# Joining the opening, the queues and the tail of an encoder kernel: seven sets of small moves

## The chip, the cores and the metric

The kernel runs on one core of a Trainium2 chip. A core has a matrix engine (TensorE, PE in the profile), VectorE (DVE), ScalarE (ACT), GpSimd (POOL) and SyncE (SP), which works in order like the others and here mostly issues DMAs. PSUM, where TensorE writes, has eight banks. The metric is device time in microseconds of one execution; less is better. The kernel before takes 2608.68 us, the median of three runs (2608.54 to 2611.68).

## The reference

The reference is one layer of a bidirectional encoder, on two sequences of 2048 tokens of width 1024 with shared weights:

- `u = rmsnorm(h)`, then one projection `z = u @ w_in` to 2304 columns, cut into q (512), k and v (128 each), attention gate `ga` (512), Fourier input `f` (512) and Fourier gate `gf` (512).
- Group A: grouped-query attention with 8 query heads and 2 key/value heads of 64, with normalised q and k and axial rotary positions, softmax over all 2048 keys, times `silu(ga)`.
- Group B: the real part of a 2-D DFT over positions and the 64 channels of each of 8 groups, then a 64 x 64 map per group, times `silu(gf)`.
- `h = h + concat(A, B) @ w_out`; then `h + (p @ w_ple) * sigmoid(rmsnorm(h) @ w_ple_gate)`, with `p` the embedded rows of width 256; a last RMS norm.

## The kernel before, in words

Products with 16-bit operands are made as three, from a high and a low half of each operand (`SPLIT3`); a value is scaled to a power of two, cast by ScalarE to its high half, and VectorE subtracts that from the value to get the low half ("split").

**Stage one, the opening (`project`, L607).** A chunk is two tiles of 128 tokens; there are 16, eight a sequence. Each `iteration(i)` (L849) holds work on several chunks at once: it loads x of chunk i+4, normalises and splits chunk i+2 (`hi_u`, `lo_u`, transposed by DMA into `uc`), projects chunk i to q and k, v (`mm_tile`), norms and rotates chunks i-1 and i-2 (`norm_q`, `rope_q`, GpSimd and VectorE), splits q and k of i-3 (`lo_q`), and between these pieces advances the sweep of chunk i-1 (`sweep_part`, the projections to f, gf and ga with their gates). Chunks other than the first of a sequence are folded: GpSimd adds the two halves of `uc` (`fold_u`), then forms sum and difference of the two tiles (`fold_s`), and ScalarE and VectorE split these (`fold_hl`) into `uf`, which the next iteration's sweep reads. Half h = 0 holds k tiles 0 to 3, half 1 the rest. Every fifth step of a sweep advances a background generator (`bg`): it scales the output weights, then the embedded rows (`embed_rows`, L440), then the channel map. Every few steps another generator, `ahead`, runs the first row maxima of the attention (`maxima(..., first=True)`, L1318), each with two PSUM banks of its own. All engines run in the order in which the text writes them.

`vs` holds v of a chunk in two buffers. `late` (L722) takes its maximum and puts its store on the list `stores_next`, which the start of the next iteration issues on SP together with the stores of the transposed q and k.

**Stage two, the attention.** 64 units of 128 queries and one key/value head, eight steps each: scores, exponentials on ScalarE (L1302), sums of these on GpSimd (L1305, L1307), a row maximum 14 steps ahead on VectorE (L1337), values (L1365); at the fifth step of the next unit the sums are made (L1381) and divided (L1388). Between the steps `interleave` puts as much of a filler as a budget in us allows: the second DFT stage with the channel map (`fourier2`), then the output stage. `mix_scale` finds the scale of the output stage, once for each sequence. `hook` (L1937) loads output weights, at every other one of its calls. In this stage all but GpSimd run in the order of the text; GpSimd's order is a planner's, by costs and readiness.

**Stage three, the output (`outp`).** For each tile t: `out1` (the product with `w_out`, two column groups), `out3` (the gate product, two groups), `middle` (squares and norm), `out2` and `out4` (the split for the gate, the last norm and store). In `slot` (L1586) a group is held: its products are made with the upper 64 rows of the array while the lower 64 rows finish the group before. From t = 30 on (`WHOLE`) a group is made at once, after the held one has been finished with the lower rows alone. A copy of one column into `seen` makes TensorE wait for what has been written. What the filler has not done when the attention ends is drained with PSUM's banks regrouped (`psD`), and there the planner orders all engines. Tile 31 needs the last unit's result, which goes to memory and comes back as `ag`.

Of the kernel before, what the change touches and what calls it, by code (L numbers as in the profile page):

```python
# [10 lines left out]
F32 = mybir.dt.float32  # L11
# [154 lines left out]
class Build:  # L166
# [146 lines left out]
    def mul1(self, name, a, b):  # L313
        t = self.keep(name, [128, 1])
        self.nc.vector.tensor_tensor(out=t[:], in0=a, in1=b, op=ALU.mult)
        return t
# [123 lines left out]
    def embed_rows(self, pool):  # L440
# [12 lines left out]

        load(0)
        yield
        load(1)
        yield
        for i in range(NT):
            load(i + 2)
            x, b = tl.pop(i), self.pb[:, 2 * i:2 * i + 2]  # L460
            nc.vector.tensor_reduce(out=b, in_=x[:], op=ALU.max, axis=AX.X, apply_absolute_value=True)
            nc.vector.tensor_scalar(out=b, in0=b, scalar1=1e-30, scalar2=None, op0=ALU.max)
            nc.vector.tensor_scalar(out=b.bitcast(I32), in0=b.bitcast(I32), scalar1=0x7F800000,
                                    scalar2=None, op0=ALU.bitwise_and)
            f = st.tile([128, 2], F32, name="p_f")
            nc.vector.tensor_scalar(out=f[:].bitcast(I32), in0=b.bitcast(I32), scalar1=-1,
                                    scalar2=(254 + W_EXP) << 23, op0=ALU.mult, op1=ALU.add)
            yield
# [138 lines left out]
    def project(self, P, PU, W, early, later, wkv, wq, wf, wgf, wga, bg, mid):  # L607
# [99 lines left out]
        def mm_tile(i, tt):  # L707
# [14 lines left out]
            def late():  # L722
                nc.vector.tensor_reduce(out=self.vmax[s][:, t:t + 1], in_=pkv[:, 128:256], op=ALU.max, axis=AX.X,
                                        apply_absolute_value=True)
                stores_next.append(lambda: nc.sync.dma_start(
                    self.vd[s][:, :, t, :].rearrange("v p d -> p v d"), vs[:, tt]))
            VL[i, tt] = late

        def norm_q(i, rs):
            rope_tables(i)  # L730
            QN[i] = qn = P.tile([128, CH, 10, 64], F32, name="qn", bufs=1)
            nc.gpsimd.tensor_tensor(out=qn[:], in0=Z[i][0][:], in1=rs[:].unsqueeze(3).to_broadcast([128, CH, 10, 64]),
                                    op=ALU.mult)
            T1[i] = t1 = P.tile([128, CH, 10, 64], F32, name="t1", bufs=2)
            rt = RT[i]
            for _, sl, nh, g in heads:
                nc.gpsimd.tensor_tensor(out=t1[:, :, sl, :], in0=qn[:, :, sl, :],
                                        in1=rt[:, g, :, 0:64].unsqueeze(2).to_broadcast([128, CH, nh, 64]),
# [1279 lines left out]
```

## Time and profile before

| | |
|---|---|
| median of three runs | 2608.68 us |
| profiled execution | 2608.45 us |
| its span, first to last instruction | 2606.7 us |
| TensorE busy | 2513.0 us, 96% |
| VectorE, ScalarE, GpSimd busy | 65%, 45%, 72% |
| mean granted TensorE clock | 0.990 |
| the opening, about | 0 to 766 us |
| attention with its fillers, about | 766 to 2512 us |
| what is left of the output stage, about | 2512 to 2607 us |

In a row of the timeline stand the start, the duration, the engine, the line, the operation, what is written and read, the count, and in square brackets the time for which the engine was idle before it, with what ended that wait. In a row of waits stand who waited for whom, the total in us, how often, and the longest. In a row of the windows stand, after the stretch, its length and the busy time of PE, PE's weight load, DVE, ACT and POOL, and then the granted clock, the busy share of the DMA engines and GB/s.

### The profile page before, as it was taken

How to read it: one execution, taken by the hardware profiler on the slowest of the kernel's cores; microseconds unless marked ns; L12 is line 12 of the kernel's file. 1: busy time of each engine (PE TensorE's matmuls, PEld its weight loads, DVE VectorE, ACT ScalarE, POOL GpSimd, SP SyncE). 2: the span in 40 equal slices, each digit the busy share in tenths (PEclk: the TensorE clock that was granted, in tenths of full speed). 3: DMA queues.
4: the chain of work that ended last, by engine and by line, in shares of the span. 5: the costliest groups of instructions: out<-in, count | busy, mean ns of one | idle time of the engine just before them, and what ended most of it. 6: DMA issues, size and time to landing. Idle time of an engine off the chain costs nothing. (4 is left out here: it accounts for less than half of the span.)

```text
span 2606.7 us, 49785 instructions
## 1 busy us (share of the span) xinstructions
PE 2513.0 (96%) x19896; PEld 1384.8 (53%) x19896; DVE 1707.0 (65%) x2318; ACT 1183.6 (45%) x1983; POOL 1879.2 (72%) x1570
## 2 busy tenths in 40 slices
PE   6999999999889999999999999999999999999998
PEld 3566666666556545545545455444544555545543
DVE  7877676887566856566676666566666666666534
ACT  4443444343235545555444455544544444444531
POOL 1466454555549988888889888887888988888850
PEclk9999999999999999999999999999999999999999
DMA  8467697876267732222222323322223222232322
GB/s 258 102 183 190 196 247 212 197 169 174 87 178 243 222 116 59 61 64 74 68 70 69 80 65 99 88 60 78 70 74 84 72 68 70 66 82 74 80 77 51
DMA packets 450601, 297.92 MB, mean 114 GB/s; under 512 B 294000, under 2 KB 394736, under 8 KB 450368
## 3 DMA queue, kind: packets, MB, share of 16 engines
q1 hardware_dynamic: 438512, 257.00, 38.3%
q0 software_dynamic: 11856, 37.74, 4.0%
q8 instruction: 155, 2.54, 0.4%
q14 instruction: 78, 0.64, 0.1%
HBM read 146.12 MB, written 82.45 MB: 88 GB/s over the span
## 5 line engine op out<-in xcount | busy, mean ns | idle before, releaser
L1307 POOL TENSOR_TENSOR acc<-acc,p 128x1024 f32<-128x1024 f32 x384 | 929.2, 2420 | 112.9 <-ACT p L1302 86.6
L1337 DVE TENSOR_REDUCE a_mx<-ps_m 128x1 f32<-128x1024 f32 x498 | 608.9, 1223 | 515.8 <-PE ps_m L1329 504.4
L1302 ACT ACTIVATE p<-ps_s,s_scale 128x512 f32<-128x512 f32 x1024 | 648.1, 684 | 641.0 <-PE ps_s L1299 628.0
L1626 PE MATMUL ps_g<-w_pg,hT 64*128 64x512 f16 x2784 | 496.5, 377 | 5.9 <-DVE seen L1592 5.4
L1365 PE MATMUL ps_o<-p,v 128*64 128x256 f32 x4096 | 468.2, 381 | 0.0
L1299 PE MATMUL ps_s<-q,k 64*128 64x512 f16 x3072 | 432.0, 377 | 1.4 <-ACT p L1302 1.0
L1365 PEld LDWEIGHTS ps_o<-p,v 128*64 128x64 f32 x4096 | 283.7, 137 | 160.0 <-issue 28.1
L491 PEld LDWEIGHTS <-uc 128*128 128x128 f16 x2400 | 235.8, 98 | 230.9 <-DMA uc<-hl 20.0
L1626 PEld LDWEIGHTS <-hT 64*128 64x128 f16 x2784 | 205.2, 94 | 160.4 <-issue 19.9
L1626 PE MATMUL ps_g<-w_wo,mh 64*128 64x512 f16 x1440 | 260.3, 376 | 2.8 <-DVE mh L1536 1.5
L1626 PE MATMUL ps_g<-w_wo,mT 64*128 64x512 f16 x1440 | 257.4, 376 | 0.2 <-DMA mT<-mh 0.2
L1299 PEld LDWEIGHTS <-k 64*128 64x128 f16 x3072 | 152.6, 94 | 194.8 <-issue 76.2
L1329 PE MATMUL ps_m<-k,q 64*128 64x512 f16 x996 | 200.5, 377 | 16.0 <-DVE a_mx L1337 15.9
L491 PEld LDWEIGHTS <-w_ga 128*128 128x128 f16 x1536 | 152.4, 100 | 45.9 <-issue 22.6
L1305 POOL TENSOR_TENSOR acc<-p,p 128x1024 f32<-128x1024 f32 x64 | 151.0, 2359 | 17.2 <-ACT p L1302 16.5
L1626 PEld LDWEIGHTS <-mh 64*128 64x128 f16 x1440 | 101.6, 94 | 91.1 <-issue 16.8
L1626 PEld LDWEIGHTS <-mT 64*128 64x128 f16 x1440 | 107.1, 94 | 76.6 <-issue 4.8
L754 POOL TENSOR_TENSOR t<-t,t 128x1280 f32<-128x1280 f32 x16 | 46.2, 2889 | 114.2 <-DVE t L750 114.2
L491 PE MATMUL ps_x<-uc,w_ga 128*128 128x256 f16 x1008 | 116.2, 276 | 4.4 <-DVE a_mx L1337 3.3
L1388 DVE RECIPROCAL ps_f<-ps_f 128x256 f32<-128x256 f32 x62 | 108.9, 1756 | 13.6 <-PE ps_f L1381 13.6
L491 PE MATMUL ps_x<-w_gf,uc 128*128 128x512 f16 x480 | 105.9, 379 | 2.5 <-DVE a_mx L1337 2.5
L1073 POOL DMA_DIRECT2D agd<-gat x64 | 35.3, 552 | 101.2 <-DVE gat L1083 96.4
(336 smaller groups left out, 3424.5 us busy)
## 6 DMA issues: line engine op xcount, KB each, us to landing
q<-qTd SPq DMA_DIRECT2D x256, 64.0 KB, 2.2
ag<-agd SPq DMA_DIRECT2D x64, 256.0 KB, 3.3
out<-h POOLq DMA_DIRECT2D x31, 512.0 KB, 3.1
x<-in_x_prompt SPq DMA_DIRECT2D x16, 512.0 KB, 4.7
gfd<-gt POOLq DMA_DIRECT2D x32, 256.0 KB, 2.6
agd<-gat POOLq DMA_DIRECT2D x64, 128.0 KB, 3.0
w_st<-in_w_out SPq DMA_DIRECT2D x32, 256.0 KB, 4.0
w_st<-in_w_ple_gate SPq DMA_DIRECT2D x32, 256.0 KB, 4.1
```

The lines of the kernel that those rows point to most:

```text
L491: self.nc.tensor.matmul(ps, lhs(ia, k), rhs(ib, k), start=(i == 0), stop=(i == 3 * ks - 1))
L754: nc.gpsimd.tensor_tensor(out=t1[:], in0=t1[:], in1=t2[:], op=ALU.add)
L1073: nc.gpsimd.dma_start(self.agd[s][1, r * 128:(r + 1) * 128, c * n:(c + 1) * n], gt[:, :n])
L1299: nc.tensor.matmul(S[u][e][:], w[sl], q[sl].rearrange("p h q -> p (h q)"), start=j == i == 0, stop=i + 1 == len(todo), skip_group_check=True)
L1302: nc.scalar.activation(p[:, e, :], S[u][e][:], AF.Exp, scale=self.sc["s_scale"][:])
L1305: nc.gpsimd.tensor_tensor(out=ACC[u][:], in0=P[u, 0][:], in1=p[:], op=ALU.add)
L1307: nc.gpsimd.tensor_tensor(out=ACC[u][:], in0=ACC[u][:], in1=p[:], op=ALU.add)
L1329: nc.tensor.matmul(ps[c], Q[u][0][sl, h, :], kt[s, kv, half][sl, :, 0, :], start=True, stop=True)
L1337: nc.vector.reduce_max(MX[u][:, h, half, c:c + 1], x, axis=AX.X)
L1365: nc.tensor.matmul(o[64 * f:64 * f + 64], vt[s, kv, c // 8][:, c % 8, :], p[:, e, f], start=(c == 0), stop=(c == 15))
L1388: nc.vector.reciprocal(r, r)
L1626: nc.tensor.matmul(g[0][:], g[1](ia, k)[sl], g[2](ib, k)[sl], start=a, stop=z, skip_group_check=True)
```

## The change

- `embed_rows`: the scale of a step's rows is made one step ahead (`scale(i + 1)`), in operations on one column instead of two; the transpose is issued a step after the low half.
- `late`: from chunk 2 on the store of v is issued at once; the second tile's is at the start of the iteration, ahead of the loads.
- `norm_q`, `rope_q`, `fold_u`: GpSimd's operations over a chunk are made tile by tile.
- `iteration`: half 0 of the folded rows is split after 12 instead of 8 us of sweep, half 1 after all of it. In the last iteration the stores of q and k are issued on GpSimd's queue (before, the switch came after them).
- `sweep_ga`: the last chunk's gates are made in the place of the k/v weights, which are done with.
- `maxima`: the first memset is on VectorE. `mul1` and one line of `mix_scale` become tensor-scalar operations.
- attention: the last unit's sums go to the bank of the maxima. `hook` loads nothing in its first four calls.
- `slot`: where a group is made whole, it comes before the rest of the held one. `norm`: on VectorE from step 512 on. `prep`: tile 31 is split after the products of tile 30.

```
 mul1:
-        self.nc.vector.tensor_tensor(out=t[:], in0=a, in1=b, op=ALU.mult)
+        self.nc.vector.tensor_scalar(out=t[:], in0=a, scalar1=b, scalar2=None, op0=ALU.mult)
 embed_rows:
+        def scale(i):
+            x, b = tl[i], self.pb[:, 2 * i:2 * i + 2]
+            nc.vector.tensor_reduce(out=b, in_=x[:], op=ALU.max, axis=AX.X, apply_absolute_value=True)
+            f = st.tile([128, 2], F32, name="p_f", bufs=2)
+            cs = [(b[:, t:t + 1], f[:, t:t + 1]) for t in range(2)]
...
+        scale(0)
+        yield
         for i in range(NT):
             load(i + 2)
-            x, b = tl.pop(i), self.pb[:, 2 * i:2 * i + 2]
...
+            x, f = tl.pop(i), fs.pop(i)
             hl = pool.tile([128, 2, 2, 256], F16, name="p_hl", tag="w2k", bufs=self.nw2k)
             for t in range(2):
                 nc.scalar.activation(hl[:, t, 0, :], x[:, t, :], AF.Copy, scale=f[:, t:t + 1])
             yield
+            if i + 1 < NT:
+                scale(i + 1)
...
+            yield
             pT = pool.tile([128, 2, 4, 128], F16, name="p_T", tag="w2k", bufs=self.nw2k)
 mm_tile, late:
-                stores_next.append(lambda: nc.sync.dma_start(
-                    self.vd[s][:, :, t, :].rearrange("v p d -> p v d"), vs[:, tt]))
+                store = lambda: nc.sync.dma_start(self.vd[s][:, :, t, :].rearrange("v p d -> p v d"), vs[:, tt])
+                if i < 2:
+                    stores_next.append(store)
+                else:
+                    store()
 norm_q:
-            nc.gpsimd.tensor_tensor(out=qn[:], in0=Z[i][0][:], in1=rs[:].unsqueeze(3).to_broadcast([128, CH, 10, 64]),
-                                    op=ALU.mult)
+            for tt in range(CH):
+                nc.gpsimd.tensor_tensor(out=qn[:, tt], in0=Z[i][0][:, tt], op=ALU.mult,
+                                        in1=rs[:, tt].unsqueeze(2).to_broadcast([128, 10, 64]))
...
 rope_q:
-            nc.gpsimd.tensor_tensor(out=t1[:], in0=t1[:], in1=t2[:], op=ALU.add)
+            for tt in range(CH):
+                nc.gpsimd.tensor_tensor(out=t1[:, tt], in0=t1[:, tt], in1=t2[:, tt], op=ALU.add)
 fold_u:
-            nc.gpsimd.tensor_tensor(out=FT[h][:], in0=x(0), in1=x(1), op=ALU.add)
+            for tt in range(CH):
+                x = [U[i][:, tt, b, 4 * h:4 * h + 4, :].rearrange("p k r -> p (k r)") for b in range(2)]
+                nc.gpsimd.tensor_tensor(out=FT[h][:, tt], in0=x[0], in1=x[1], op=ALU.add)
 iteration:
+            if ok(i - 1) and i > 2:
+                VL.pop((i - 1, 1))()
+            if i == n + 3:
+                self.last_stores = nc.gpsimd
             if ok(i + 4):
                 load_x(i + 4, 0)
...
-            if ok(i - 1) and i > 2:
-                VL.pop((i - 1, 1))()
...
                 fold_u(i, 1)
-                sweep_part(8.0)
+                sweep_part(12.0)
                 fold_hl(i, 0)
                 fold_s(i, 1)
-                sweep_part(7.0)
+            sweep_part(1000.0 if i < n else (6.0, 9.0, 5.0, 100.0)[i - n])
+            if folds(i):
                 fold_hl(i, 1)
-            sweep_part(1000.0 if i < n else (6.0, 9.0, 5.0, 100.0)[i - n])
 sweep_ga:
+        g8 = self.gat8() if (s, c) == (1, NT // 2 - 1) else None
-            gt = w2k("gat")
+            gt, th = (w2k("gat")[:, :n], w2k("th")) if g8 is None else (g8[:, 2 * r], g8[:, 2 * r + 1])
 maxima:
-                    nc.gpsimd.memset(MX[u][:], -3e38)
+                    nc.vector.memset(MX[u][:], -3e38)
 attention:
-                    ps = self.bank()
+                    ps = self.bank() if u < n else self.psM.tile([128, 1024], F32, name="ps_m")
 mix_scale:
-        nc.vector.tensor_tensor(out=b[:], in0=b[:], in1=mm[:, 2:3], op=ALU.max)
+        nc.vector.tensor_scalar(out=b[:], in0=b[:], scalar1=mm[:, 2:3], scalar2=None, op0=ALU.max)
 slot:
-            if low is not None and (low[4] or whole):
+            def seen():
                 j = st.tile([128, 1], F32, name="seen")
                 nc.vector.tensor_copy(j[:], low[0][:, 0:1])
+            if low is not None and low[4] and not whole:
+                seen()
...
-            if low is not None:
-                yield from halves(None, low)
             if up is not None:
                 ps = self.group_bank()
                 for i, us in enumerate(self.mm(ps[:], up[0], up[1])):
                     yield us
                     yield from embed(i >= 6)
+                if low is not None:
+                    seen()
                 yield from self.after(ticket)
                 yield from end(up[2](ps))
+            if low is not None:
+                yield from halves(None, low)
 norm:
-            e = nc.vector if self.dq is None or t == 0 else nc.gpsimd
+            e = nc.vector if self.dq is None or t == 0 or self.step >= 16 * N2 else nc.gpsimd
 prep:
-            while MB == 1 and t - 1 in M:
+            while (MB == 1 and t - 1 in M) or (t == N2 - 1 and not free):
                 yield None
 outp:
+                if t == N2 - 2:
+                    free.append(True)
 run:
-                    W[n] = A.tile([128, 2, 8, cols[n][1] - cols[n][0]], F16, name="wr_" + n)
+                    W[n] = A.tile([128, 2, 8, cols[n][1] - cols[n][0]], F16, name="wr_" + n, tag="wr_" + n)
+                self.gat8 = lambda: A.tile([128, 8, 256], F32, name="gat8", tag="wr_kv")
 hook:
-                    for _ in range(n if n > 1 else len(calls) % 2):
+                    for _ in range(n if n > 1 else len(calls) % 2 if len(calls) > 4 else 0):
```

More of the change, by code (lines that the diff above doesn't have):

```diff
@@ L452, in load @@
                 nc.sync.dma_start(tl[i][:], src[2 * i // NT][:, j:j + 2, :])
+        def scale(i):
[3 more added lines that the diff above has]
+            cs = [(b[:, t:t + 1], f[:, t:t + 1]) for t in range(2)]
+            for x, _ in cs:
+                nc.vector.tensor_scalar(out=x, in0=x, scalar1=1e-30, scalar2=None, op0=ALU.max)
+            for x, _ in cs:
+                nc.vector.tensor_scalar(out=x.bitcast(I32), in0=x.bitcast(I32), scalar1=0x7F800000,
+                                        scalar2=None, op0=ALU.bitwise_and)
+            for x, y in cs:
+                nc.vector.tensor_scalar(out=y.bitcast(I32), in0=x.bitcast(I32), scalar1=-1,
+                                        scalar2=(254 + W_EXP) << 23, op0=ALU.mult, op1=ALU.add)
+            fs[i] = f
+        fs = {}
         load(0)
@@ L731, in norm_q @@
             QN[i] = qn = P.tile([128, CH, 10, 64], F32, name="qn", bufs=1)
[L732 to L733 removed]
+            for tt in range(CH):
+                nc.gpsimd.tensor_tensor(out=qn[:, tt], in0=Z[i][0][:, tt], op=ALU.mult,
+                                        in1=rs[:, tt].unsqueeze(2).to_broadcast([128, 10, 64]))
             T1[i] = t1 = P.tile([128, CH, 10, 64], F32, name="t1", bufs=2)
             rt = RT[i]
[L736 to L739 removed]
+            for tt in range(CH):
+                for _, sl, nh, g in heads:
+                    nc.gpsimd.tensor_tensor(out=t1[:, tt, sl, :], in0=qn[:, tt, sl, :], op=ALU.mult,
+                                            in1=rt[:, g, tt, 0:64].unsqueeze(1).to_broadcast([128, nh, 64]))
             del Z[i]
@@ L906, in iteration @@
                 self.drain(self.ahead)
-                self.last_stores = nc.gpsimd
-                for f in stores_next:
-                    f()
-                del stores_next[:]
         both = lambda f, i: [f(i, tt) for tt in range(CH)]
@@ L1067, in sweep_ga @@
                                lambda b, k: uc[:, :, b, k, :], n)
-            gt = w2k("gat")
+            gt, th = (w2k("gat")[:, :n], w2k("th")) if g8 is None else (g8[:, 2 * r], g8[:, 2 * r + 1])
             def more(r=r, gt=gt):
-                nc.vector.tensor_reduce(out=self.tmax[s][:, c * 4 + r:c * 4 + r + 1], in_=gt[:, :n], op=ALU.max,
+                nc.vector.tensor_reduce(out=self.tmax[s][:, c * 4 + r:c * 4 + r + 1], in_=gt, op=ALU.max,
                                         axis=AX.X, apply_absolute_value=True)
-                nc.gpsimd.dma_start(self.agd[s][1, r * 128:(r + 1) * 128, c * n:(c + 1) * n], gt[:, :n])
-            self.silu2(gt[:, :n], ps[:, :n], self.sc["h_ga"], w2k("th"), more)
+                nc.gpsimd.dma_start(self.agd[s][1, r * 128:(r + 1) * 128, c * n:(c + 1) * n], gt)
+            self.silu2(gt, ps[:, :n], self.sc["h_ga"], th, more)
     def silu2(self, out, z, half, th, then):
@@ L1770, in outp @@
         ticket = [-1]
-        todo, held, started, due, tm, tk, t4 = [], [], [], [], [], {}, {}
+        todo, held, started, due, tm, free, tk, t4 = [], [], [], [], [], [], {}, {}
         self.grouped = True
```

11 lines of the change are left out of this document (1 added, 10 removed).

## The prediction

> **What bounds the kernel now.** I read the page first, then the waits of TensorE, then the clock in the stretches behind its longest waits.
>
> ```profile
> span 2606.7 us, 49785 instructions
> ...
> PE 2513.0 (96%) x19896; PEld 1384.8 (53%) x19896; DVE 1707.0 (65%) x2318; ACT 1183.6 (45%) x1983; POOL 1879.2 (72%) x1570
> ...
> POOL 1466454555549988888889888887888988888850
> ```
>
> TensorE is busy 2513.0 of 2606.7 us. None of the edits takes matmuls away, so all that can be won lies in the 93.7 us in which it is idle, and in busy time at a lowered clock. The profiled execution took 2608.45 us, 1.75 more than its span, and the median of the runs shown is 2608.68; the sum below is made against 2608.45.
>
> ```profile
> PE ps_m L1329 <- DVE a_mx L1337: 15.9, 22, 2.6
> PE ps_x L1329 <- DVE a_mx L1337: 6.6, 1, 6.6
> PE ps_g L1626 <- DVE seen L1592: 6.5, 2, 5.4
> PE ps_x L491 <- DVE a_mx L1337: 5.8, 2, 3.3
> PE ps_g L1012 <- ACT ft L1007: 5.0, 1, 5.0
> PE ps_x L1012 <- ACT ft L1007: 3.5, 2, 2.4
> PE ps_g L1155 <- DMA bd<-bdd: 2.1, 1, 2.1
> PE ps_g L1209 <- DMA g_in<-gd: 1.9, 1, 1.9
> ```
>
> Columns: total us, times, longest. The reader is to see few, long waits at single places, and that each of them ends on another engine's queue, not on TensorE's own work.
>
> ```profile
> 520.30:526.90 6.60, 6.58 (x27) 4.07 (x28) 6.50 (x7) 0.55 (x1) 6.45 (x5) 0.54 0.21 40
> 662.20:667.30 5.10, 5.10 (x27) 3.40 (x26) 3.03 (x5) 0.21 (x1) 3.57 (x4) 0.59 0.30 108
> 752.90:760.90 8.00, 7.99 (x49) 6.13 (x49) 5.23 (x10) 2.15 (x4) 5.13 (x6) 0.65 0.83 247
> 2524.90:2533.80 8.90, 8.88 (x21) 2.70 (x20) 0.00 (x0) 0.02 (x1) 1.26 (x1) 0.52 0.80 236
> ```
>
> The third number from the right is the granted clock. Behind a long wait it is down, and TensorE loses (1 - clock) of the stretch: 6.60 x 0.46 = 3.0, 5.10 x 0.41 = 2.1, 8.00 x 0.35 = 2.8, and 8.90 x 0.48 = 4.3 us. A wait that goes takes this with it.
>
> [...]
>
> **The change part by part.**
>
> (a), (b) Values' store at once; scales of the embedded rows one step ahead.
>
> ```profile
> 511.41 0.28 ACT L720 ACTIVATE vs<-ps_x 128x128 f32<-128x128 f32 x1 [5.54 <-DMA vd<-vs]
> ...
> 518.79 0.91 ACT L471 ACTIVATE p_hl<-p_in,p_f 128x256 f16<-128x256 f32 x2 [7.10 <-DVE p_f L466]
> 520.32 2.07 PE L1012 MATMUL ps_g<-ft,dft 128*128 128x512 f32 x2 [5.00 <-ACT ft L1007]
> ```
>
> ```profile
> ACT vs L720 <- DMA vd<-vs: 69.6, 11, 10.9
> ```
>
> ```profile
> L466 DVE TENSOR_SCALAR p_f<-pb x16: 169/170/2189, 433.0 to 608.3; 128x2 int32<-128x2 int32 x16
> ```
>
> ScalarE works in order. It held `vs` for a buffer whose store had been put off by an iteration (5.54), then the rows' scaling for a factor that VectorE had not yet made (7.10; L466 takes 0.17 us as a rule and 2.19 at worst), and TensorE's first-stage matmul stood behind both. In all L720 waited 69.6 us for stores. The store now leaves an iteration earlier, so L720 has nothing to wait for. On SP it stands ahead of the iteration's x and rope loads, whose readers come later in the iteration or in the next. The factor is made one step ahead, so L471 finds it done. Three small VectorE operations become six, 16 times: 48 x 0.17 = 8 us from 433 to 608 us, beside TensorE's work; without that cover they would cost these 8. So (a) the two earlier waits on `ft`, 3.5, which end behind the same store; bounds 0 to 3.5, taken whole, since nothing else stood between. Below nothing none of the terms (a) to (f) goes by itself, for each takes an operation out of a queue, shortens it or starts it earlier; what may wait anew is in the rivals. (b) 5.0 + 3.0 = 8.0; bounds 0 to 8.0, taken whole.
>
> (c) The maxima's memset on VectorE.
>
> ```profile
> 660.85 0.13 POOL L1333 MEMSET a_mx<- 128x16 f32 x1
> 661.01 1.29 DVE L1337 TENSOR_REDUCE a_mx<-ps_x 128x1 f32<-128x512 f32 x2 [8.17 <-POOL a_mx L1333]
> ```
>
> 0.13 us of memset sat behind GpSimd's folds, VectorE idled 8.17 us for it, and TensorE 6.6 for VectorE. On VectorE it runs where its reader runs. Next late would be ScalarE's tanh, for which TensorE has other banks. 6.6 + 2.1 = 8.7; bounds 0 to 8.7, taken whole.
>
> (d) GpSimd's work in halves.
>
> ```profile
> L737 POOL TENSOR_TENSOR t<-qn,rt 128x1024 f32<-128x1024 f32 x16 | 39.7, 2481 | 1.3
> L737 POOL TENSOR_TENSOR t<-qn,rt 128x256 f32<-128x256 f32 x16 | 12.6, 788 | 0.0
> ```
>
> From these, 1024 elements in 2481 and 256 in 788 ns, a piece costs 2.2 ns an element and 0.22 us of its own. A chunk gets six pieces more (one in the norm, two in the products, one in the rotation's sum, two in the folds): 1.3 us, 21 us in 16 chunks. The page's POOL digits, 4 to 6 tenths in slices 2 to 12 (up to 780 us), are the cover; at the nine tenths of the later slices all of it would be paid. What it may bring is that VectorE gets its turn sooner. That matters where TensorE waits for VectorE at the end of the opening: 5.8 + 2.8 = 8.6, bounds 0 to 8.6. Most of VectorE's queue there is its own work, so I take 2.0.
>
> [...]
>
> (e) Last stores on GpSimd's queue, last gates in kv's weights, output weights loaded from the fifth call on.
>
> ```profile
> 766.39 0.37 SPq L791 DMA_DIRECT2D kTd<-kT  x1
> ...
> 767.01 1.89 SPq L1186 DMA_DIRECT2D bd<-bdd  x1
> ```
>
> SP came to `bd` behind three stores; TensorE waited 2.1 for `bd` and 1.9 for `g_in`. Three issues less, and two weight loads fewer ahead of `g_in`, bring both forward. GpSimd's gate stores queue behind the three moved ones, and their tiles no longer hold the next stage's space. Bounds 0 to 4.0, I take 3.0.
>
> (f) Small VectorE operations as tensor-scalar.
>
> ```profile
> L1472 DVE TENSOR_TENSOR mxb<-mxb,mx4s x2: 1455/2026/2596, 867.3 to 1322.9; 128x1 f32<-128x1 f32 x2
> L1470 DVE TENSOR_SCALAR mxb<-mx4s,va_i x2: 273/273/273, 867.0 to 1322.6; 128x1 f32<-128x1 f32 x2
> ```
>
> ```profile
> 872.46 0.39 PE L1329 MATMUL ps_m<-k,q 64*128 64x512 f16 x2 [2.61 <-DVE a_mx L1337]
> ```
>
> ```profile
> PE ps_m L1329 <- DVE a_mx L1337: 1.6, 2, 1.0
> ```
>
> One column takes 1.5 to 2.6 us as tensor-tensor and 0.27 as tensor-scalar. Both mixes delay the maxima's reduction and TensorE behind it, by 2.6 and (waits from 1320 to 1340) 1.6 us. Bounds 0 to 4.2, I take 4.0.
>
> (g) The tail: whole group ahead of the held half, last norm on VectorE, last sums in the free bank, split 31 held back.
>
> ```profile
> 97.76 5.35 PE L491 MATMUL ps_x<-wr_q,uc 128*128 128x512 f16 x24 [1.36 <-DMA uc<-hl]
> ```
>
> ```profile
> 2512.24 1.25 PE L491 MATMUL ps_x<-w_wo,mh 128*128 128x512 f16 x5
> 2514.43 0.19 POOL L1653 TENSOR_SCALAR h_ms<-h_ss 128x2 f32<-128x2 f32 x1 [2.62 <-ACT h_hl L1647]
> 2518.84 1.32 POOL L1656 TENSOR_SCALAR h_r<-rsh_z 128x1 f32<-128x1 f32 x1
> 2524.92 6.55 PE L1626 MATMUL ps_g<-w_pg,hT 64*128 64x512 f16 x15 [5.37 <-DVE seen L1592]
> ...
> 2549.37 0.17 DVE L1653 TENSOR_SCALAR h_ms<-h_ss 128x2 f32<-128x2 f32 x1 [1.22 <-ACT h_hl L1647]
> 2551.74 0.15 DVE L1656 TENSOR_SCALAR h_r<-rsh_z 128x1 f32<-128x1 f32 x1
> ```
>
> The norm takes 20.16 - 14.43 = 5.7 us on GpSimd and 2.5 on VectorE, so all behind it is 3.2 earlier. The whole group's operands are there at 2512.24; its 24 matmuls (5.35 us, as the first row shows for 24 of this kind) fill the 5.37 us of the wait for `seen`, and the clock stays up: 5.4 + 4.3 = 9.7. The second whole group covers the last chunk's chain. Lower bound 3.2, if only the norm counts, upper 9.7; a loss is excluded because the work put ahead needs nothing that is late. I take 9.5.
>
> Sum: 3.5 + 8.0 + 8.7 + 2.0 + 3.0 + 4.0 + 9.5 = 38.7. Against it two new waits of the common kind, 15.9 / 22 = 0.7 us each. 2608.45 - 38.7 + 1.4 = **2571 us**, 1.4% less.
>
> **The rivals.** One: other waits of the opening step in. L471 may stand behind its own load or buffer, VectorE may now wait for a load one step earlier. For it: the opening's engines are 4 to 6 tenths busy but coupled by one buffer each. Against: TensorE had no wait there but those named. Half of (b) and (c), all of (d) and (e) gone: 2571 + 8.4 + 5.0 = 2584.
>
> Two: the tail's order doesn't come out so, as the planner and not the text orders it there and may place the held half first again. For it: five matmuls of the whole group were already placed early and the rest was not. Then only the norm's 3.2 remains of (g): 2571 + 6.3 = 2577; with rival one 2590.
>
> Three, slower: the second half of the folded rows is split only after the whole sweep, and the next chunk's folded matmuls reach it before it is there.
>
> ```profile
> ACT uf L827 <- POOL f_s L820: 46.8, 13, 13.8
> ```
>
> ```profile
> L827 ACT ACTIVATE uf<-f_s x28: 1039/1052/1058, 96.5 to 719.7; 128x1024 f16<-128x1024 f32 x28
> ```
>
> ```profile
> 102.95 2.78 PE L491 MATMUL ps_x<-wr_kv,uc 128*128 128x256 f16 x24
> ```
>
> TensorE has two projections, 2 x (5.35 + 2.78) = 16.3 us, between the sweep's end and that half. ScalarE's worst wait for the folds was 13.8, and 1.05 for the split comes on top, which speaks for it; that the fold has some 4 us of sweep more to be done in speaks against. There are 28 / 2 = 14 such chunks. It makes the kernel slower once each is 37.5 / 14 = 2.7 us late; at 3.5 us it is 2571 + 49 = 2620.
>
> **How the numbers follow.** Forecast 0.56; rival one 0.17, rival two 0.14 (both together within these), all faster by over 0.2%, which is 5.2 us and about what a measurement of this kernel can tell from no change: 0.87. Rival three 0.07. Gains and new waits cancelling within 0.2%: 0.06. Low end: all upper bounds, 3.5 + 8.0 + 8.7 + 8.6 + 4.0 + 4.2 + 9.7 = 46.7, give 2562, and some four of the 0.7 us waits less 2559. High end: (a) to (c) gone, 20.2, and rival two, 2571 + 26.5 = 2597.
>
> **What would show it.** Right: no wait on `ft` or on `vd` stores; no 6.6 us wait at the first maxima; no wait on `seen`, the clock at 1.00 through the tail, and the whole group's 24 matmuls ahead of the held half; L1472 at 0.3 us; `bd` and `g_in` off TensorE's list; TensorE's idle time near 65 us. Wrong: new waits of TensorE on `uf`, on `uc` or on loads in the opening; a busy sum above 2513 with the clock still down; idle time above 80 us.

## The result, and the profile after

The changed kernel takes 2597.87 us (median of five runs, 2592.75 to 2601.59), the kernel before 2611.45 us (2608.54 to 2616.09): ratio 0.9949, 95% interval 0.993 to 0.9967. It is faster, as forecast, but by 13.6 us instead of 37.5, and lies just above the upper end of the range. The profiled execution took 2597.87 us, its span is 2595.8 us, 10.9 less than before. The page of the changed kernel begins:

```profile
span 2595.8 us, 49879 instructions
...
PE 2511.0 (97%) x19896; PEld 1384.0 (53%) x19896; DVE 1668.4 (64%) x2382; ACT 1183.6 (46%) x1983; POOL 1896.6 (73%) x1646
```

TensorE is idle for 2595.8 - 2511.0 = 84.8 us, 8.9 less than before, where I had named 65 as right and over 80 as wrong. The waits of TensorE in the changed kernel:

```profile
PE ps_s L1317 <- ACT p L1320: 5.9, 6, 4.0
PE ps_g L1056 <- ACT uf L846: 5.1, 2, 3.6
PE ps_g L504 <- DVE h L1570: 4.9, 1, 4.9
...
PE ps_x L504 <- DVE a_mx L1355: 3.8, 2, 2.4
PE ps_g L1649 <- DVE seen L1610: 3.6, 2, 2.4
PE ps_g L1173 <- DMA bd<-bdd: 2.2, 1, 2.2
PE ps_x L1056 <- ACT uf L846: 2.1, 2, 1.5
...
PE ps_x L1056 <- DVE uf L847: 1.9, 2, 1.1
...
PE ps_x L1029 <- ACT ft L1024: 1.4, 1, 1.4
...
PE ps_g L1056 <- DVE uf L847: 1.3, 2, 0.7
...
PE ps_g L1227 <- DMA g_in<-gd: 0.2, 1, 0.2
```

In this execution the 6.6 us at the first maxima, the 5.0 us on `ft` at 520 us and all but 0.2 of the wait for `g_in` are gone. The second is gone in all executions with this edit; the first and the third are not, as the part on right and wrong says. New are four rows on `uf`, 5.1 + 2.1 + 1.9 + 1.3 = 10.4 us, and 4.9 us on `h` in the tail. The stretches behind three of the `uf` waits, with the granted clock third from the right:

```profile
284.30:290.00 5.70, 5.01 (x28) 3.36 (x29) 4.79 (x7) 5.67 (x11) 0.68 (x2) 0.70 0.57 140
330.90:338.00 7.10, 6.31 (x33) 3.88 (x34) 6.30 (x10) 7.04 (x13) 0.54 (x1) 0.76 0.82 212
379.80:386.00 6.20, 5.53 (x30) 3.65 (x31) 5.27 (x8) 6.17 (x11) 0.30 (x1) 0.72 0.59 135
```

By estimate each loses a further 1.7 us: 5.70 x 0.30, 7.10 x 0.24, 6.20 x 0.28. (The matmuls agree: 20 folded ones take 3.89 us at 285.60 us, and 24 take 2.78 at 280.06, ahead of the wait.) So late `uf` costs 10.4 + 5.1 = 15.5 us.

Where the time went is read best from TensorE's own milestones. The table gives, for one profiled execution of each kernel, how much later (+) or earlier (-) than in the kernel before a stage begins; chunk c begins with its first k, v matmul, unit 0 with the first matmul of the attention, and "values end" is the last matmul of the attention's values. The names of the experiments are those of the next section.

```
us against the kernel before   changed   e1     e2     e9     e7    e10    e12
chunk 3                          +1.0   +0.9   +1.2   +1.5   +0.8   -0.2   +0.5
chunk 6                          +3.0   +0.9   +1.3   +1.5   +0.8   -0.2   +0.5
chunk 8                         +10.0   +7.8   +3.0   +8.8   -0.5   -0.8   -0.8
chunk 11                        +13.5   +9.7  +12.2  +13.1   -0.7   +5.0   +0.8
chunk 12                         +5.2   +1.4   +8.0  +11.5   -8.9   -3.2   -7.4
chunk 15                         -4.1   -0.6  +10.6  +12.2  -11.1  -12.7  -16.9
unit 0                           -7.1   -0.8   +9.4   +9.2  -13.9  -15.4  -19.6
unit 6                          -10.7   -6.9  +13.7  +11.2  -16.7  -17.5  -21.8
unit 9                           -8.9   -7.3  +11.2   +8.1  -16.5  -17.3  -21.9
values end                      -11.8   -8.2   +9.5   +9.7  -17.7  -18.4  -23.2
end                             -10.9   -8.8   +9.4   +9.8  -23.5  -24.2  -28.8
```

The changed kernel loses 13.5 us up to chunk 11, wins 8.3 at the old stall of 515 us, 9.3 at the first maxima, 3.0 to the attention's begin and 4.7 in the attention, and gives 0.9 back in the tail. Each column is one execution. e3 and e4 of the next section have the changed kernel's opening unaltered: their chunk 11 is 13.7 and 13.5 us late, so that entry can be relied on, but their unit 0 is 3.3 and 3.5 us early instead of 7.1, so the entries behind it are good to some 4 us only.

### The profile page after: what moved, and what is told of

It is laid out like the page before. It is cut to its first block, busy times and chain, and to the rows that moved or that the text cites. A ratio compares the mean times of both kernels' runs of the same rounds, so it can differ in the third digit from the quotient of the medians.

```text
span 2595.8 us, 49879 instructions
## 1 busy us (share of the span) xinstructions
PE 2511.0 (97%) x19896; PEld 1384.0 (53%) x19896; DVE 1668.4 (64%) x2382; ACT 1183.6 (46%) x1983; POOL 1896.6 (73%) x1646
## 5 line engine op out<-in xcount | busy, mean ns | idle before, releaser
L772 POOL TENSOR_TENSOR t<-t,t 128x640 f32<-128x640 f32 x32 | 49.2, 1556 | 121.2 <-DVE t L767 121.2
L1406 DVE RECIPROCAL ps_f<-ps_f 128x256 f32<-128x256 f32 x61 | 107.1, 1756 | 13.6 <-PE ps_f L1399 13.6
L1390 ACT ACTIVATE at<-ps_o,a_scale 128x256 f32<-128x256 f32 x64 | 30.4, 474 | 168.2 <-PE ps_o L1383 168.2
```

Source lines behind the costliest of these rows:

```text
L772: nc.gpsimd.tensor_tensor(out=t1[:, tt], in0=t1[:, tt], in1=t2[:, tt], op=ALU.add)
L1390: nc.scalar.activation(at[:].rearrange("p c q -> p (c q)"), o, AF.Copy, scale=self.sc["a_scale"][:])
L1406: nc.vector.reciprocal(r, r)
```

## The experiments

All ratios are to the kernel before, with 95% intervals; the diffs are against the changed kernel where nothing else is said.

**e1: the folds' places as before.**

```
-                sweep_part(12.0)
+                sweep_part(8.0)
                 fold_hl(i, 0)
                 fold_s(i, 1)
-            sweep_part(1000.0 ...)
-            if folds(i):
+                sweep_part(7.0)
                 fold_hl(i, 1)
+            sweep_part(1000.0 ...)
```

> The changed kernel with the places of fold_hl and the sweep's 8 and 7 us as they were before; all else as changed. Theory A (the later split of the folded rows costs what the opening lost): TensorE's waits on uf (10.4 us in the profile of the changed kernel, with some 5 us of lowered clock behind three of them) go, the milestones of chunks 3 to 11, 1.0 to 13.5 us behind the kernel before, stand 0 to 3.5 us ahead of it, and the time is 2597.9 - 15 = 2583 us, ratio to before 0.989. Theory B (the folded rows are late for another reason, GpSimd's halves or the stores at once): the waits on uf stay and the time is 2598, ratio 0.995. Theory C (the two halves were put later because ScalarE would otherwise hold tanh and ft behind them): uf goes, waits on ft come back, 3.5 us with the clock behind them, and the time is 2587 to 2590.

Measured: 2598.23 us, ratio 0.9946 (0.9929 to 0.9964), the same as with them. Of the 13.5 us lost at chunk 11, 9.7 stay, and a wait of 4.3 us is back at the first maxima. Theory A alone is false: something else makes the folds late too, and their later place also gains something further on.

**e2: only the later folds**, on the kernel before (the diff of e1, the other way).

> The kernel before with the later fold_hl (sweep 12 us, second half after the whole sweep) and nothing else of the change. Theory A: the waits on uf come here too, chunk 11 begins some 13 us later than before, and the time is 2608.7 + 13 = 2622 us, ratio 1.005. Theory B (it needs GpSimd's halves to be late): no wait on uf, ratio 1.000 +- 0.001. If the stall of 515 us (ScalarE behind p_f) absorbs a late start, the loss at the attention's begin is less than the loss at chunk 11.

Measured: 2617.35 us, ratio 1.0024 (1.0014 to 1.0035): slower by 6.3 us. Chunk 11 is 12.2 us late, of which the stall at 515 us takes in 4.2. So the later folds do cost, as theory A says, though only a part of what it put down to them.

**e3: the tail as before** (`slot`, `norm`, `prep` and the bank of the last sums; the diff is the last part of the change's, the other way).

> The changed kernel with slot, norm, prep and the last sums' bank as before. Theory D (the tail's four edits are worth nothing, because the wait for seen was replaced by one for h behind the split of tile 31): ratio to before 0.995 as with them, time within 2 us of the changed kernel's, and the wait of 5.4 us on seen is back. Theory E (they gain, and the tail of the changed kernel is long for an unrelated reason): the time is 5 to 10 us above the changed kernel's, ratio 0.997 to 0.999.

Measured: 2597.37 us, ratio 0.9949 (0.9933 to 0.9965), and the wait is back:

```profile
PE ps_g L1644 <- DVE seen L1610: 6.5, 2, 5.3
```

Theory D holds: four edits that I had put at 9.5 us change nothing that this can tell.

**e4: the split of tile 31 behind the addition of tile 30.** Its scale is copied by an operation that also reads a column which that addition has written, so the planner can't place it ahead.

```
             def low():
-                nc.vector.scalar_tensor_tensor(out=mh[:, 1], in0=ag, scalar=msc[:], in1=mh[:, 0],
+                m2 = msc
+                if t == N2 - 1:
+                    m2 = st.tile([128, 1], F32, name="m2")
+                    nc.vector.scalar_tensor_tensor(out=m2[:], in0=X[t - 1][:, 0:1], scalar=0.0, in1=msc[:],
+                                                   op0=ALU.mult, op1=ALU.add)
+                nc.vector.scalar_tensor_tensor(out=mh[:, 1], in0=ag, scalar=m2[:], in1=mh[:, 0],
```

> The changed kernel, with the low half of tile 31 made to read a column that out1's first group of tile 30 has written, so that VectorE's queue holds that group's addition ahead of it. Theory D: the 4.9 us wait of TensorE on h goes, and with it the lowered clock behind it (12.5 us of matmuls at 0.5 to 0.7): 6 to 8 us less than the changed kernel, ratio to before 0.992. Theory F (the chain through memory to tile 31 sets the end, and TensorE would wait for it a little later): the wait appears at the next group, and the time is within 2 us of the changed kernel's.

Measured: 2589.58 us, ratio 0.9921 (0.9905 to 0.9936), 8.3 us below the changed kernel's median; in the profiles the way from the attention's last value matmul to the end is 94.6 us against 101.0 (and 100.0 before). Over all profiles it is 94.2 to 96.3 us with this order (six kernels), 99.4 to 104.1 with the changed tail and 99.9 to 103.2 with the tail of before. The timelines show the place. In the changed kernel, TensorE first and then VectorE:

```profile
2509.87 0.80 PE L1649 MATMUL ps_g<-w_pg,hT 64*128 64x512 f16 x3 [2.42 <-DVE seen L1610]
2510.60 4.45 PE L504 MATMUL ps_g<-w_wo,mh 128*128 128x512 f16 x12
2514.89 2.75 PE L504 MATMUL ps_g<-w_wo,mT 128*128 128x512 f16 x12
2517.58 1.68 PE L1649 MATMUL ps_g<-w_pg,hT 64*128 64x512 f16 x7
2524.14 2.72 PE L504 MATMUL ps_g<-wp,pT 128*128 128x512 f16 x6 [4.88 <-DVE h L1570]
```

```profile
2522.14 1.28 DVE L1554 SCALAR_TENSOR_TENSOR mh<-ag,mix_s,mh 128x1024 f16<-128x1024 f32 x1 [12.33 <-ACT mh L1549]
2523.34 0.74 DVE L1570 SCALAR_TENSOR_TENSOR h<-ps_g,mixo,h 128x512 f32<-128x512 f32 x1
```

and in e4:

```profile
2518.83 0.75 DVE L1575 SCALAR_TENSOR_TENSOR h<-ps_g,mixo,h 128x512 f32<-128x512 f32 x1 [7.87 <-PE ps_g L504]
...
2522.55 1.28 DVE L1559 SCALAR_TENSOR_TENSOR mh<-ag,m,mh 128x1024 f16<-128x1024 f32 x1 [2.78 <-ACT mh L1549]
```

In the changed kernel VectorE stands for 12.33 us at the split of tile 31, which waits for the last unit's way through memory; the addition L1570, whose matmuls had ended at 2517.6, stands behind it, and TensorE waits for the bank that L1570 reads. With the order turned the addition runs at 2518.83, and TensorE goes on.

**e5: v's second store behind the loads**, with the folds' places as in e1.

```
-            if ok(i - 1) and i > 2:
-                VL.pop((i - 1, 1))()
             if i == n + 3:
...
             del stores[:]
+            if ok(i - 1) and i > 2:
+                VL.pop((i - 1, 1))()
```

> The changed kernel with the folds' places of before (as in e1) and the second tile's store of v behind the loads of x and rope and the stores of q and k on SP, where it stood before, but still at once. Theory G (the store ahead of the loads delays rope's landing, 4.8 us before and 5.6 to 6.1 in e1, GpSimd's rope and folds start later by that, and the loop GpSimd, ScalarE, VectorE, SP, GpSimd carries it into the next chunk): rope lands in 5.0 us again, the waits on uf at chunks 7 and 8 go, chunk 9 begins within 2 us of the kernel before instead of 7.9 behind it, and the time is 2598.2 - 6 = 2592, ratio 0.992. Theory H (GpSimd's halves are the delay): nothing moves, ratio 0.9946.

Measured: 2596.96 us, ratio 0.9946 (0.9934 to 0.9958), as e1. Chunk 9 is 7.0 us late instead of 7.9, and rope lands as late as in e1 (5.5 to 7.1 us after its issue from the third chunk to the seventh). Theory G is not the cause of the delay; a share of a microsecond isn't excluded.

**e6: GpSimd's operations whole**, with the folds' places as in e1. In `norm_q`, `rope_q` and `fold_u` the loops over the two tiles are one operation again.

```
-            for tt in range(CH):
-                nc.gpsimd.tensor_tensor(out=t1[:, tt], in0=t1[:, tt], in1=t2[:, tt], op=ALU.add)
+            nc.gpsimd.tensor_tensor(out=t1[:], in0=t1[:], in1=t2[:], op=ALU.add)
```

> The changed kernel with the folds' places of before (as in e1) and GpSimd's operations whole again (norm_q, rope_q, fold_u); the store of v stays ahead of the loads. Theory G: the waits on uf stay, chunk 9 begins 6 to 8 us behind the kernel before, ratio 0.994 to 0.995. Theory H: GpSimd gains about 1 us in each chunk, the waits on uf go, ratio 0.992. Beside it: if the halves gave VectorE its turn sooner at 743 and 752 us, the two waits of 2.4 and 3.0 us there become 2.5 and 3.3 us again.

Measured: 2592.89 us, ratio 0.9932 (0.9916 to 0.9949). Chunk 9 is 1.5 us ahead of the kernel before where e1 was 7.9 behind it, unit 0 14.4 us ahead where e1 was 0.8. Theory H is right: the halves are most of the delay, though 1.8 us of waits on `uf` stay. What was expected beside it missed: the two waits at 743 and 752 us are 2.5 and 1.6, not 2.5 and 3.3.

**e7: folds' places, store and whole operations of before, with e4's order in the tail.**

> The changed kernel with the folds' places, the place of v's store and GpSimd's whole operations of before, and the split of tile 31 behind the addition as in e4. If G and H both have a share, the opening keeps the gains at 515 and 655 us without the loss ahead of them: 2598.2 - 10 (chunk 9 not behind the kernel before) - 7.3 (the tail, as e4 showed) = 2581 us, ratio 0.9885. If the loss has another cause, the tail alone: 2591, ratio 0.992.

Measured: 2585.40 us, ratio 0.9897 (0.9884 to 0.991). That lies between the two expectations. The opening no longer loses, but a wait is back at the first maxima: TensorE, then VectorE.

```profile
656.67 0.58 PE L1344 MATMUL ps_x<-k,q 64*128 64x512 f16 x1 [4.57 <-DVE a_mx L1352]
```

```profile
653.86 2.16 DVE L844 TENSOR_TENSOR uf<-f_s,uf 128x1024 f16<-128x1024 f32 x1 [7.58 <-ACT uf L843]
655.94 1.28 DVE L1352 TENSOR_REDUCE a_mx<-ps_x 128x1 f32<-128x512 f32 x2
```

The memset runs on VectorE, yet VectorE stands for 7.58 us at the split of the first half of the folded rows, for GpSimd's sum, and the maximum stands behind it.

**e8: e4 with v's second store behind the loads** (e4's and e5's edits without e1's).

> e4 (split of tile 31 behind the addition) with v's store behind the loads and nothing else taken back: the later folds and the halves stay. Theory G, if it explains the whole loss: chunk 9 begins within 3 us of the kernel before, time 2589.6 - 10 = 2580, ratio 0.988. If the later folds have a share of their own, which e2 points to (8 us behind at chunk 9 with them alone): the waits on uf stay in part, 2586 to 2589, ratio 0.991 to 0.992.

Measured: 2589.07 us, ratio 0.9913 (0.99 to 0.9927), not to be told from e4. Theory G had expected chunk 9 within 3 us of the kernel before; it is 9.7 us late, against 13.5 in e4. So the store's place doesn't explain the loss; a share of up to 3.8 us, in one execution each, isn't excluded, but the times don't show it.

**e9: only the halves**, on the kernel before (the diff of e6, the other way).

> The kernel before with GpSimd's operations in halves (norm_q, rope_q, fold_u) and nothing else of the change. Theory H (a pass of GpSimd from norm to the last fold is 16.4 us whole and 18.0 in halves, and that is on the loop that feeds uf): the pass is 18.0 us here too, the margin of uf at chunks 5 to 8, 4.0, 3.4 and 1.6 us in the kernel before, falls below nothing, waits on uf appear at about 330 and 380 us, chunk 9 begins 4 to 8 us later than before, ratio 1.001 to 1.003. Rival (halves hurt only together with the store or the factor made ahead): no wait on uf, ratio 1.000.

Measured: 2618.25 us, ratio 1.0028 (1.0017 to 1.004): slower by 7.3 us, nearly all of it in the opening. A pass of GpSimd over one chunk in the kernel before, from the norm to the last fold:

```profile
203.87 2.33 POOL L732 TENSOR_TENSOR qn<-z,q_rs 128x1280 f32<-128x1280 f32 x1 [0.80 <-DVE q_rs L673]
206.28 3.03 POOL L737 TENSOR_TENSOR t<-qn,rt 128x1024 f32<-128x1024 f32 x2
209.27 2.12 POOL L814 TENSOR_TENSOR f_t<-uc 128x1024 f32<-128x1024 f16 x1
...
214.06 2.12 POOL L814 TENSOR_TENSOR f_t<-uc 128x1024 f32<-128x1024 f16 x1
...
217.80 2.50 POOL L820 TENSOR_TENSOR f_s<-f_t 128x512 f32<-128x512 f32 x2
```

and the same pass in halves:

```profile
209.35 2.48 POOL L733 TENSOR_TENSOR qn<-z,q_rs 128x640 f32<-128x640 f32 x2 [0.24 <-DVE q_rs L673]
211.79 3.32 POOL L739 TENSOR_TENSOR t<-qn,rt 128x512 f32<-128x512 f32 x4
215.07 2.26 POOL L817 TENSOR_TENSOR f_t<-uc 128x512 f32<-128x512 f16 x2
...
220.00 3.28 POOL L817 TENSOR_TENSOR f_t<-uc 128x512 f32<-128x512 f16 x2
...
224.89 2.51 POOL L823 TENSOR_TENSOR f_s<-f_t 128x512 f32<-128x512 f32 x2
```

It takes 220.30 - 203.87 = 16.4 us whole and 227.40 - 209.35 = 18.0 in halves. Four of the extra pieces (norm, products, first fold) cost 0.6 us together, 0.14 each. Most of the rest is in the last fold, 3.28 us instead of 2.12. VectorE's split at the same time, first whole and then in halves:

```profile
215.10 2.16 DVE L828 TENSOR_TENSOR uf<-f_s,uf 128x1024 f16<-128x1024 f32 x1 [1.52 <-ACT uf L827]
```

```profile
221.04 1.23 DVE L831 TENSOR_TENSOR uf<-f_s,uf 128x1024 f16<-128x1024 f32 x1 [2.21 <-ACT uf L830]
```

Beside the whole fold VectorE's split takes 2.16 us and lasts until 1.1 us after the fold's end at 216.18; in halves it takes 1.23 us and runs within the fold's 3.28. The first fold of that pass takes 2.26 us, and so does the last one at 220.15 us in the changed kernel, where no split runs beside it (VectorE's is at 227.05). So the last fold is 1.0 us longer with the split beside it; that the split runs between the two pieces is my reading. VectorE gains 0.9 us, about what GpSimd loses.

And the pass begins 5.5 us later, while TensorE's chunk begins only 1.5 us later; four passes in a row begin 1.6, 2.5, 5.5 and 5.0 us later. In the kernel before they are 36.2, 36.7 and 39.3 us apart and TensorE's chunks 42.5, so that GpSimd gets ahead from chunk to chunk; in halves it gets ahead more slowly. That each pass waits for the one before it, by way of ScalarE, VectorE and the loads, is read from the order of the text and not traced step by step. The time that the second half of the folded rows is finished ahead of its first matmul (that of the start of the f matmuls plus 2.6 us, half of them; below nothing it is a wait), for the folded chunks in order:

```
folded chunk      2     3     4     5     6     7
before          1.2   7.3  12.6   4.0   3.4   1.6
e9              0.6   4.8   6.3  -2.0   5.2   0.3
e1              0.6   4.9   7.1  -1.9  -3.9  -3.1
e7              0.6   7.2  12.4   4.2   3.2  -1.2
e10             1.1   5.1   9.4   2.6  -1.2  -6.5
changed        -2.5   3.3   6.6  -2.9  -3.0  -5.0
```

The margin grows to 12.6 us at the fourth chunk, and then a reduction on GpSimd (last section) takes most of it. Halves take 6 us off the fourth, later folds 3, both 6; the fifth, sixth and seventh had 4.0, 3.4 and 1.6 to give. These are single executions: with the changed kernel's opening, e3 and e4 have 0.3 and 2.1 at the fifth and -5.3 and -3.3 at the sixth. With both causes out, e6, e7 and e12 still have -1.2 to -2.9 at the seventh; what else of the change takes that is open.

The expectation of e9 was right in the time and missed the places: of the waits on `uf` there is one of 1.3 us, at the fifth chunk. The rest of the loss goes by `ft`, whose waits are 11.8 us against 8.5 before, 3.8 of them at 300 us and 3.7 at 392, and by the clock. And it ends there: from chunk 9 to chunk 11 e9 stays 13.1 us behind, and the margins of the second sequence are above nothing in every profile. The same pieces cost nothing more in that sequence.

**e10: e4 with GpSimd's operations whole** (the later folds stay).

> The changed kernel with GpSimd's operations whole, and the split of tile 31 behind the addition; the later folds and the store stay. Theory: the folds' lateness adds to the halves' (margin at chunk 7: 1.6 before, -5.0 in the changed kernel, -3.1 with the folds back, -2.6 with both back). With the later folds and whole operations the waits on uf at 325 and 372 us stay, as in e2, some 4 to 6 us with the clock, but the wait of 4.6 us at the first maxima that e7 has (VectorE stands behind the first half's folds there) does not: u0 within 3 us of e7's, ratio 0.989 to 0.991. If the later folds cost nothing by themselves: 2581, ratio 0.9885.

Measured: 2584.38 us, ratio 0.9903 (0.9887 to 0.9918), 5.2 us below e4. The later folds' own price is left:

```profile
PE ps_g L1053 <- ACT uf L843: 5.1, 1, 5.1
```

That is folded chunk 7. There is no wait at the first maxima. How the second half comes to be late, at the same chunk in the changed kernel, on ScalarE:

```profile
368.98 0.72 ACT L434 ACTIVATE w_o<-w_st,wf_s 128x512 f16<-128x512 f32 x1 [4.17 <-DMA w_st<-in_w_out]
369.61 1.04 ACT L846 ACTIVATE uf<-f_s 128x1024 f16<-128x1024 f32 x1
...
378.34 0.47 ACT L1099 ACTIVATE th<-ps_x,h_ga 128x256 f32<-128x256 f32 x1 [2.88 <-DMA agd<-gat]
378.71 1.05 ACT L846 ACTIVATE uf<-f_s 128x1024 f16<-128x1024 f32 x1
```

The first half stands behind a weight's scaling that waits 4.17 us for its load. GpSimd's second sum needs the first half's buffer and ends at 375.0. The second half stands behind the last gate, which waits 2.88 us for a store, and begins 3.7 us after its sum.

**e11: as e10, with the second half after 7 us of sweep, as before.**

> As e10, but with the second half's split after 7 us more of sweep, as before, and the first half's after 12 us, as changed. If it is the first half's place that frees VectorE for the maxima and the second half's that makes TensorE wait, this has neither: no 4 us wait at 655 us and no wait over 1.5 us on uf, 3 to 6 us less than e7: 2580, ratio 0.988. If the first half's place alone makes GpSimd late, since the second sum needs its buffer: waits on uf as in e10.

Measured: 2583.33 us, ratio 0.9899 (0.9884 to 0.9915), not to be told from e10 or e7. The wait on `uf` at folded chunk 7 stays (5.6 us), as the expectation's other branch has it, and at the first maxima 1.0 us is left of 4.6. But the second half did not get the place that it had before: after 12 and 7 us of sweep it still stands behind the last gate, where it stands in e10.

```profile
369.70 0.47 ACT L1096 ACTIVATE th<-ps_x,h_ga 128x256 f32<-128x256 f32 x1 [2.96 <-DMA agd<-gat]
```

The split follows at 370.07, as in e10 at 369.44; in the kernel before it runs at 362.00, ahead of that gate. GpSimd's sum ends at 366.3 here and at 356.0 in the kernel before. Of the 8 us by which the split is later, then, some 4 come from the late sum, which waits for the first half's buffer and ends 4.3 us after the split's old start, and some 4 from the place behind the gate. e11 doesn't tell the two halves' places apart.

**e12: e10, with the folds' early places up to iteration 11 and the later ones from 12 on.**

```
+                late_ = i >= 12
-                sweep_part(12.0)
+                sweep_part(12.0 if late_ else 8.0)
                 fold_hl(i, 0)
                 fold_s(i, 1)
+                if not late_:
+                    sweep_part(7.0)
+                    fold_hl(i, 1)
             sweep_part(1000.0 ...)
-            if folds(i):
+            if folds(i) and late_:
                 fold_hl(i, 1)
```

> As e7 (GpSimd's operations whole, split of tile 31 behind the addition, v's store ahead of the loads as changed), with the folds' early places up to iteration 11 and the changed, later ones from iteration 12 on. If the early place only hurts where the attention's first maxima stand in VectorE's queue behind it (the wait of 4.6 us at 657 us in e7, 4.0 in e6), and the late place only hurts before that (5.1 us at 371 us in e10): neither wait, chunk 12 begins 8 to 9 us ahead of the kernel before, u0 18 to 21 us, time 2578 to 2581 us, ratio 0.987 to 0.988. If the wait of 657 us comes from something else that moves with the earlier chunks: as e7, 2585, ratio 0.9897.

Measured: 2580.00 us, ratio 0.9871 (0.9854 to 0.9887). It beats both kernels, by 32.2 us the one before (2612.24 in this comparison) and by 17.9 us the changed one. Both waits are gone or small, as forecast: 2.1 us on `uf` in all, none at the first maxima. Unit 0 is 19.6 us ahead, within what was expected; chunk 12 is 7.4 ahead, a little less than the 8 to 9. Its page:

```profile
span 2577.8 us, 49833 instructions
...
PE 2503.6 (97%) x19896; PEld 1382.6 (54%) x19896; DVE 1672.9 (65%) x2383; ACT 1183.0 (46%) x1983; POOL 1875.0 (73%) x1554
```

TensorE is idle for 74.2 us.

## Why the prediction was right or wrong

By the milestones of the profiled executions, against 38.7 us less 1.4 for new waits:

| term | forecast | measured |
|---|---|---|
| (a) stores at once, up to chunk 11 | 3.5 | -13.5 |
| (b) stall at 515 us | 8.0 | 8.3 |
| (c) first maxima | 8.7 | 9.3 |
| (d) 743 and 753 us | 2.0 | 3.0 |
| (e) and (f) the attention | 7.0 | 4.7 |
| (g) tail | 9.5 | -0.9 |
| sum | 38.7 | 10.9 |

**Two steps failed, and they are nearly all of the 27.8 us.** The first is the cover in (d): "The page's POOL digits, 4 to 6 tenths in slices 2 to 12, are the cover". The 1.3 us a chunk that I took off the halves' rows measured 1.6, but the agreement is luck: the pieces that I priced cost 0.14 us and not 0.22, and some 1.0 us is in the last fold, which takes 3.28 us with VectorE's split beside it and 2.26 without. That GpSimd's idle time would hide it was wrong: e9, which has the halves alone, is 7.3 us slower, and taking them out gives 5.3 (e6) and 5.2 us (e10) back. Each of GpSimd's passes in the opening feeds the splits of ScalarE and VectorE and, by way of these, the next pass. What covers a longer pass there is not GpSimd's idle share but the margin with which `uf` and `ft` reach TensorE. That margin has to grow by GpSimd's getting ahead, and it is 4.0, 3.4 and 1.6 us at the chunks that decide. From chunk 9 on, where the margin is larger again, the halves took nothing more. I had ScalarE's waits for the folds, 46.8 us in 13, as a row in the prediction, and that row was the sign that work on GpSimd could reach ScalarE.

The second half of this failure is that the later folds had no term in the sum. They were in the third rival only, with a chance of 0.07 and a common price for 14 chunks. What that rival names came, together with the halves, at four places: `uf` late by 1.7, 2.2, 2.3 and 4.3 us, 10.4 in all, with the clock 15.5. The argument against it, that "the fold has some 4 us of sweep more to be done in", overlooked two things: GpSimd's second sum waits for the first half's buffer, so a later first half moves the second sum back with it; and the second half's split comes to stand behind the last gate on ScalarE, 3.7 us after its sum in the changed kernel. 3.5 gained on `ft`, 1.4 lost there at 122 us and 15.5 on `uf` give -13.4, what the milestones show. e9 and e2 price the two causes alone at 7.3 and 6.3 us.

**(g)** The wait did move as the norm's part said: `seen` came 5.37 - 2.42 = 3.0 us earlier, against 3.2 forecast. But "a loss is excluded because the work put ahead needs nothing that is late" looked at TensorE's queue only. What became late next was on VectorE: its split of tile 31 was placed ahead of the whole group's addition, and the 5.4 us at `seen` became 2.4 + 4.9 at two places, each with a lowered clock behind it, 7.7 us at 0.78 and 6.4 us at 0.70:

```profile
2509.90:2517.60 7.70, 7.70 (x28) 2.88 (x28) 0.00 (x0) 0.00 (x0) 0.00 (x0) 0.78 1.02 269
2524.10:2530.50 6.40, 6.36 (x21) 2.10 (x21) 1.45 (x2) 0.00 (x0) 0.00 (x0) 0.70 0.11 21
```

That the planner would not do as the text says was rival two. In part its order came as I named it, for three matmuls of the held half still stand ahead of the whole group and wait for `seen` (the row at 2509.87); what cost more is an order that I did not name. `prep` was to hold the split back, and in the order of the text it does; why the planner put it first no run shows. With the split held back, e4's tail is 5.4 us shorter than that of the kernel before, of the 9.5 forecast, and e4 takes 8.3 us less than the changed kernel.

**(b)** was right in mechanism and size: the wait on `p_f` ahead of the first-stage matmul at 520 us is gone and no lowered clock follows there. Elsewhere ScalarE still waits for `p_f`, 23.6 us in 4 waits against 54.5 in 9 before, but TensorE waits behind none of them. **(c)** was half right in reason, and its size is in part luck. The memset's move alone leaves 2.3 to 4.6 us of the 6.6 (e1, e5, e6, e7), since VectorE then stands at the first half's split. With the halves of the rows split later the rest goes in the changed kernel, e10 and e12, and 0.4 is left in e8; but e3 and e4, with the same opening as the changed kernel, keep 2.0 us there, and gain 5.7 and 5.8 us from chunk 12 to chunk 15 where the changed kernel gains 9.3. So the later folds cost in the first eleven chunks and gain in the last ones, which e12 turns to use.

**(d)** is open. The second wait is 1.4 to 1.7 us in the changed kernel, e3 to e10 and e12 and 3.0 to 3.3 in the kernel before, e1, e2 and e11, with halves and with whole operations on both sides; the halves don't decide it, and I don't know what does. The 2.0 us for VectorE's getting its turn sooner were my estimate, and no run shows them. What e9 shows in that pass is VectorE's split 0.9 us shorter and GpSimd's last fold 1.0 us longer.

**(e), (f)** (e) is not shown. `bd` stayed at 2.2 us, and the fall of `g_in` from 1.9 to 0.2 is this execution's: with the same edit it is 0.3 to 2.7 us in the experiments. (f) holds, at about its forecast: the small operations went from 1.46 to 2.60 us to 0.21, and 1.9 and 1.8 us came off at their places (units 3 to 6 and 18 to 21); e3, e4 and e12 show the same, 1.5 to 2.0 at each. Then 1.8 us were lost between units 6 and 9, at a place of which the last section tells.

## What to carry to other kernels

An engine's idle share does not say whether its work is hidden. Where engines wait for each other in a ring, work added to one of them is paid out of the margin with which the ring's product reaches the bound engine; here GpSimd was 4 to 6 tenths busy and 1.6 us more a round cost 7.3 us in all, at the chunks where the margin was 4 us or less, and nothing in the second sequence, where it was 6 us or more. Before work is called free, list for each consumer, round by round, by how many us its operand was early. And when a wait is taken away by a new order, look at the queues of all engines behind it: in this tail the next thing late stood in front of the freed work on another engine. There a planner placed the operations, and a real dependence held the split back (e4) where the order of the text had not.

## What the runs showed of the hardware

GpSimd's reduction over partitions takes 0.4 us by its row, but GpSimd does nothing for 6.0 us before it and, once it has issued the stores that follow, for 7.2 to 8.1 us more, with no wait in the profile. In the kernel before, between 200 and 300 us (the first row is 7.6 in the changed kernel and 8.1 in e9):

```profile
POOL f_s L820 <- issue: 7.2, 1, 7.2
POOL wf_mm L407 <- issue: 6.0, 1, 6.0
```

The pass that holds it is 30 to 33 us long instead of 16.4, and the fifth folded chunk, which it feeds, has a margin of 4.0 us even in the kernel before, where the one ahead of it has 12.6. It is one of the places where the changed kernel waits. What either idle time is, the profile doesn't say.

Two operations of a short chain on VectorE took 1.18 and 2.27 us instead of 0.16 beside two of GpSimd's. The first tile's norm, 0.16 us an operation, in the changed kernel:

```profile
952.58 0.16 DVE L274 TENSOR_TENSOR rsh_t<-rsh_z 128x2 f32<-128x2 f32 x1
952.77 1.18 DVE L275 TENSOR_TENSOR rsh_t<-rsh_t,rsh_hx 128x2 f32<-128x2 f32 x1
953.98 2.27 DVE L279 SCALAR_TENSOR_TENSOR rsh_z<-rsh_t,rsh_z 128x2 f32<-128x2 f32 x1
```

GpSimd at the same time, and TensorE after it:

```profile
952.67 1.27 POOL L1535 TENSOR_TENSOR ag<-ag 128x512 f32<-128x512 f32 x1 [0.95 <-DVE rsh_z L279]
953.89 2.34 POOL L1325 TENSOR_TENSOR acc<-acc,p 128x1024 f32<-128x1024 f32 x1
```

```profile
959.09 1.16 PE L1317 MATMUL ps_s<-mr,kone 64*128 64x512 f16 x2 [4.01 <-ACT p L1320]
```

They end, at 953.95 and 956.25 us, when the two operations of GpSimd end. ScalarE waits for the norm ahead of its exponentials, and TensorE for these, 4.0 of the 5.9 us in the first row of the waits. This is one execution: at the same place TensorE waits 1.9 us in e5, and not over 0.9 in the other experiments. A like case in the kernel before: L466, 0.17 us as a rule, takes 2.05 us from 477.51 us on and ends at 479.56, beside a fold of GpSimd that takes 2.12 and ends at 479.53. Why they end together no run shows.

The granted clock was also down behind waits shorter than those of 3.3 to 6.6 us ahead of the prediction's stretches. Two waits of some 1.5 and 0.7 us, little over a microsecond apart, were followed by a granted clock of 0.70 at 284 us and 0.76 at 331 us, and one of 2.4 us by 0.78 at 2510 us. So a wait of some 2 us had 1.7 us of clock behind it at these places (5.70 x 0.30, 7.70 x 0.22). Not everywhere: in the kernel before, waits of 2.38 us at 381.6 us and of 2.50 us at 743.5 us were followed by a granted clock of 1.00, and what decides it is open.
